# A planned decoder layer on one core: queues of tiles sorted by first use, links between real users of a tile, PSUM banks by need, and gate and value columns in one group

## The chip, the cores and the metric

The kernel runs on one core of one Trainium2 chip. The metric is the device time of one launch in microseconds. The engines are TensorE (PE), VectorE (DVE), ScalarE (ACT), GpSimd (POOL), and SyncE (SP), which issues all transfers.

## The reference, cut to what matters

One decoder layer on `x` of 2048 x 1024 float32. Two head groups share the projection `w_in`: an RG-LRU and a Conformer convolution module. Then come `w_out`, cross-attention into 256 memory tokens, and a gated FFN with a short convolution.

```python
h = rms_norm(x, mix_norm_g[l])
z = h @ w_in[l]                                   # 1024 x 2048
lru_x, lru_gate, conf_a, conf_b = jnp.split(z, [D_LRU, 2 * D_LRU, 2 * D_LRU + D_CONF], axis=-1)
lru_x = causal_dwconv(lru_x, lru_conv_w[l], lru_conv_b[l])
y_lru = rg_lru(lru_x, ...) * jax.nn.gelu(lru_gate, approximate=True)
c = conf_a * jax.nn.sigmoid(conf_b)               # value, gate
c = causal_dwconv(c, conf_conv_w[l], conf_conv_b[l])      # 31 taps
c = jax.nn.silu(layer_norm(c, conf_ln_g[l], conf_ln_b[l]))
x = x + jnp.concatenate([y_lru, c], axis=-1) @ w_out[l]
...
scores = jnp.einsum("bshd,bmhd->bhsm", q, k) * (XA_HD ** -0.5)
p = jax.nn.softmax(scores, axis=-1)
x = x + jnp.einsum("bhsm,bmhd->bshd", p, v).reshape(bsz, s, d) @ w_o[l]
...
x = x + (jax.nn.gelu(causal_dwconv(g, ...), approximate=True) * u) @ w_down[l]
return rms_norm(x, final_norm_g)
```

## The kernel before

The kernel is written as a program that is recorded first and ordered afterwards. Every operation (a matmul, a vector operation, a transfer) becomes an `Op` with an engine, an estimated cost, its predecessors, and the buffers it uses. Buffers are taken from pools: `S` (86 tiles of 128x512 in SBUF), `W` (4 wide tiles, which hold the raw weight columns `raw` among others), `D` (3 tiles for the 31-tap convolution), and `ps` (the 8 banks of PSUM). The recording order comes from generators (tasks such as `mix`, `channels`, `recurrences`, `attend`) that yield to each other.

`emit` then plans in `PASSES` rounds. `deadlines` walks the operations backwards and gives each a due time: no later than each successor's due time less the cost, and, by `extra`, no later than what the next user of the same pool slot needs. `schedule` simulates the engines forward: each engine takes the ready operation with the earliest due time, and a buffer gets a slot when one is free. The queue of each pool says whose turn is next; it stands in the order of recording. The plan with the earliest estimated end is kept, and the instructions of all engines are written in one sequence in its order. The chip runs each engine's instructions in that order. All instructions come from one helper line of `emit` (L452 before, L485 with the change), so the profile is read by the names of tiles.

Products are float32 products made of three: both operands are split into a high and a low part (`wh`, `wl`; `xh`, `xl`), and three 128x512 matmuls are added in a bank (`mm3`). The products of `w_out`, of the attention and of the FFN go by Strassen's scheme (`seven`, with the list `FIRST` for `w_out`); their combined operands are `yh`, `yl`, `s`, `Xh`, `Xl`.

The work around the change: the sequence is cut into two halves `h` of 1024 positions, of two quarters `q` of 512 each. `mix(h)` makes z for one half: `project(h, c0, put)` multiplies 256 columns of `w_in` from column `c0`, which `Columns.get` loads with `raw_cols` in two tiles of 512 rows (`kq`), and hands each finished bank to `put`. `mix_conf(h, c)` does that for the gate columns of two 128-channel blocks and then for their value columns; the sigmoid of the gate waits in `sg` tiles meanwhile, and the product goes to the DRAM tile `zc`. `channels(h)` runs the 31-tap convolution (`conv`; tiles `so`, `e`, `f`) of each channel block `c` once `got["conf", h, ...]` is done. `mix_lru` and `recurrences` do the same for the LRU (tiles `z`, `xc`, `gate`, `gelu`). `attend(h)` multiplies by `w_out`, normalises the queries and runs the softmax (tiles `prob`, `sum`, `r`, `pt`).

Of the kernel before, what the change touches and what calls it, by code (L numbers as in the profile page):

```python
# [14 lines left out]
ALU = mybir.AluOpType  # L15
AX = mybir.AxisListType

P = 128
# [35 lines left out]
ACT_SWITCH = 1.3  # L54
ACT_PATIENCE = 8.0
POOL_LAST = 6.0
PASSES = 12
BACKLOG = 4.0
EARLY_STORE = 40.0
SMALLS = 720  # L60
STACKS = 2
# [90 lines left out]

class Op:
    __slots__ = ("eng", "idx", "calls", "cost", "delay", "sets", "preds", "succs", "bufs", "due",
                 "wait", "at", "start", "either", "on", "turn", "store", "first", "early")

    def __init__(self, eng, idx):
        self.eng, self.idx = eng, idx
# [6 lines left out]
class Program:  # L165
# [94 lines left out]
    def prepare(self):  # L260

        for tag, queue in self.queues.items():
            live = []
            for b in queue:
                while live and live[0] < b.ops[0].idx:
                    heapq.heappop(live)
                heapq.heappush(live, b.ops[-1].idx)
                assert len(live) <= SLOTS[tag], tag
        for o in self.ops:
            for p in o.preds:  # L270
                p.succs.append(o)
        extra = {}
        for tag, queue in self.queues.items():
            dead = sorted(queue, key=lambda b: b.ops[-1].idx)
            for i, b in enumerate(queue[SLOTS[tag]:]):
                for u in dead[i].ops:
                    extra.setdefault(u.idx, []).append(b.ops[0])
        self.extra = extra

    def deadlines(self, order):  # L280

        t = 0.0
        for o in order:
            if o.eng == "PE":
                t = o.due = o.turn = t if o.start is None else o.start
                t += o.cost
            else:
                o.due = t + 30 if o.store else 1e9
        for o in self.ops:
            o.start, o.at = None, 0.0  # L290
        for o in reversed(self.ops):
            lat = o.cost + o.delay + HOP
            if o.early:
                o.due -= EARLY_STORE
            for s in o.succs:
                o.due = min(o.due, s.due - lat)
            for s in self.extra.get(o.idx, ()):
                if s.idx > o.idx:
                    o.due = min(o.due, s.due - lat)
            if o.first:  # L300
                o.due = o.idx - 1e6
        for _ in range(STACKS):
            for e in ("DVE", "ACT", "SP"):
                t = 1e9
                for o in sorted((o for o in self.ops if o.eng == e and not o.first), key=lambda o: -o.due):
                    t = o.due = min(o.due, t - o.cost)
            for o in reversed(self.ops):
                lat = o.cost + o.delay + HOP
                if o.eng != "PE" and not o.first:
                    for s in o.succs:  # L310
                        o.due = min(o.due, s.due - lat)

    def schedule(self):
        events, seq = [], [0]
# [8 lines left out]
        def push(t, kind, x):  # L323
            seq[0] += 1
            heapq.heappush(events, (t, seq[0], kind, x))

        def satisfied(o, t):
            o.at = max(o.at, t)
            o.wait -= 1
            if o.wait == 0:  # L330
                push(o.at, 1, o)

        def grant(tag, t):
            while free[tag] and queues[tag]:
                b = queues[tag].pop()
                b.slot = free[tag].pop(0)
                b.left = len(b.ops)
                for o in b.heads:
                    satisfied(o, t)
# [59 lines left out]

        for o in self.ops:  # L400
            o.wait = len(o.preds) + 1
        for tag, queue in self.queues.items():
            for b in queue:
                for o in b.heads:
                    o.wait += 1
        for tag in SLOTS:
            grant(tag, 0.0)
        for o in self.ops:
# [20 lines left out]
                        free[b.tag].append(b.slot)  # L429
                        grant(b.tag, t + HOP)  # L430
        assert len(order) == len(self.ops)
        self.estimated = end
        return order

    def emit(self, tc):
        self.prepare()
        best, order = None, self.ops
        for _ in range(PASSES):
            self.deadlines(order)
            order = self.schedule()  # L440
            if best is None or self.estimated < best[0]:
                best = self.estimated, order, {o.idx: (o.start, o.on) for o in order}, {id(b): b.slot for q in self.queues.values() for b in q}
        _, order, places, slots = best
        with tc.manual_schedule(engines=None):
            for o in order:
                o.start, o.on = places[o.idx]
                for b in o.bufs:
                    if b.real is None:
                        b.real = self.place(b, slots[id(b)])
                e = self.engines[o.on]  # L450
                for name, args, kw in o.calls:
                    getattr(e, name)(*[resolve(a) for a in args], **{k: resolve(a) for k, a in kw.items()})  # L452
# [27 lines left out]
def hybrid_layer(  # L480
# [44 lines left out]
    def tmp(name="tmp"):  # L525
        return pr.new("S", name=name)
# [137 lines left out]
    class Kept:  # L664
# [18 lines left out]
        def get(self, i, shape=None, name=None):  # L683
            b = pr.new("S", shape, self.dtype, name or self.name)
            self.load((b[:] if shape is None else flat(b)).f32(), i)
            return b

    def raw_cols(w, c0, kq):
        st = pr.new("W", (P, KQ, 2 * P), name="raw")
        pr.dma(st[:], w[kq * KQ * P : (kq + 1) * KQ * P, c0 : c0 + 2 * P].rearrange("(k p) f -> p k f", p=P))  # L690
        return st

    def raw_rows(w, r0):
# [13 lines left out]
    class Columns:  # L707


        def __init__(self, w, name, n, uses):  # L710
            self.w, self.kept, self.uses = w, Kept(name, n * 4) if uses > 1 else None, uses
            self.seen = {}

        def get(self, c0, kq):
            key = (c0, kq)
            n = self.seen[key] = self.seen.get(key, 0) + 1
            base = ((c0 // (2 * P)) * 2 + kq) * 4
            if n > 1:
                return [tuple(self.kept.get(base + 2 * f + i, (P, KQ, P), "w" + "hl"[i]) for i in range(2)) for f in range(2)]
            st = raw_cols(self.w, c0, kq)  # L720
            got = [split_cols(st, f) for f in range(2)]
            if n < self.uses:
                for f in range(2):
                    for i in range(2):
                        self.kept.put(base + 2 * f + i, flat(got[f][i]))
            return got
# [110 lines left out]
    def wide(name):  # L837
        return pr.new("W", (P, 2 * TT), name=name)

    got = {(n, h, c): Task(None) for n in ("conf", "lru") for h in range(NH) for c in (0, 2)}  # L840

    def project(h, c0, put):
        pp = [[ps(), ps()] for _ in range(2)]
        for kq in range(2):
            ww = W_in.get(c0, kq)
            for f in range(2):
                wh, wl = ww[f]
                for th in range(2):
                    with together():
                        for k in range(KQ):  # L850
                            x = MX[h][th][kq * KQ + k]
                            mm3(pp[f][th][:], wh[:, k, :], wl[:, k, :], x[0][:], x[1][:], kq + k == 0, kq == 1 and k == KQ - 1)
                    if kq:
                        put(f, th, pp[f][th])
                    yield 0

    def mix(h):
        parts = [mix_conf, mix_lru]
        for part in parts:
            for c in (0, 2):  # L860
                yield from part(h, c)
        mixed_in[h].done = True
        MX[h].clear()

    def mix_conf(h, c):
        sg = {}

        def gate(f, th, p):
            t = sg[f, th] = tmp("sg")
            ACT(t[:], p[:], AF.Sigmoid)  # L870

        yield from project(h, 3 * DL + c * P, gate)

        def value(f, th, p):
            t = sg[f, th]
            V("tensor_tensor", t[:], p[:], t[:], op=ALU.mult)
            zc.put(c + f, 2 * h + th, t[:])

        yield from project(h, 2 * DL + c * P, value)
        got["conf", h, c].done = True  # L880

    def mix_lru(h, c):
# [379 lines left out]
    def channels(h):  # L1262
        acc = []
        for c in range(NC4):
            yield got["conf", h, c // 2 * 2]
            out = tmp("conv"), tmp("conv")
            yield from conv(c, h, out)
            acc.append(out)
            yield 0
        for i in range(2):  # L1270
            mixed[2 * h + i] = [o[i] for o in acc]
            conf_in[2 * h + i].done = True
# [611 lines left out]
```

## Time and profile before

| | us |
|---|---|
| median of 3 runs | 2452.07 (2451.44 to 2452.39) |
| the profiled execution, its own time | 2454.62 |
| its span | 2452.8 |
| TensorE busy | 2404.8 (98%) |
| VectorE busy | 1925.6 (79%) |
| ScalarE busy | 1281.6 (52%) |
| mean granted TensorE clock | 0.993 |

The profile is of one execution. Busy times are sums over an engine's instructions; a tile's name stands for all its buffers, in the form output<-inputs. "Idle before" names what ended an engine's wait. The chain of waits is followed back from the last instruction. "SPq" is SyncE issuing a transfer.

### The profile page before, as it was taken

How to read it: one execution, taken by the hardware profiler on the slowest of the kernel's cores; microseconds unless marked ns; L12 is line 12 of the kernel's file. 1: busy time of each engine (PE TensorE's matmuls, PEld its weight loads, DVE VectorE, ACT ScalarE, POOL GpSimd, SP SyncE). 2: the span in 40 equal slices, each digit the busy share in tenths (PEclk: the TensorE clock that was granted, in tenths of full speed). 3: DMA queues.
4: the chain of work that ended last, by engine and by line, in shares of the span. 5: the costliest groups of instructions: out<-in, count | busy, mean ns of one | idle time of the engine just before them, and what ended most of it. 6: DMA issues, size and time to landing. Idle time of an engine off the chain costs nothing.

```text
span 2452.8 us, 32183 instructions
## 1 busy us (share of the span) xinstructions
PE 2404.8 (98%) x10788; PEld 1982.3 (81%) x10788; DVE 1925.6 (79%) x3231; ACT 1281.6 (52%) x2250; POOL 0.7 (0%) x6
## 2 busy tenths in 40 slices
PE   7999999999989999999999999999999999999998
PEld 6888878888767888778888888888888888888887
DVE  6489979999989646697888888988786685667666
ACT  8237677367887556675545545545454331233222
POOL 0000000000000000000000000000000000000000
PEclk9999999999989999999999999999999999999999
DMA  7998678897887967556575456654542388779774
GB/s 252 323 307 294 218 237 309 284 313 249 265 303 246 330 232 240 188 175 235 203 239 193 146 189 220 213 186 147 179 146 69 108 284 281 251 237 357 252 245 180
DMA packets 339837, 572.05 MB, mean 233 GB/s; under 512 B 32925, under 2 KB 106653, under 8 KB 339671
## 3 DMA queue, kind: packets, MB, share of 16 engines
q1 hardware_dynamic: 339670, 570.00, 68.5%
q8 instruction: 85, 1.39, 0.2%
q14 instruction: 82, 0.66, 0.1%
HBM read 385.32 MB, written 184.55 MB: 232 GB/s over the span
## 4 chain that ended last, share of the span: by engine, by line
PE 92%; DVE 3%; ACT 2%; DMA 1%; issue 1%; SPq 0%; DVEq 0%; ACTq 0%
PE ps L452 92%; ACT prob L452 1%; ACT L452 0%; DMA raw<-in_w_q_dram 0%; DVE Xl L452 0%; DVE s L452 0%; DVE acc L452 0%; DVE gate L452 0%; SPq L452 0%; DVE wl L452 0%; DVE yl L452 0%; DVE x L452 0%; DVE e L452 0%; ACT yh L452 0%; DVE conv L452 0%
## 5 line engine op out<-in xcount | busy, mean ns | idle before, releaser
L452 PE MATMUL ps<-Xh,wh 128*128 128x512 f32 x1344 | 523.9, 390 | 0.9 <-DVE gb L452 0.9
L452 PE MATMUL ps<-Xh,wl 128*128 128x512 f32 x1344 | 523.1, 389 | 0.3 <-DVE wl L452 0.3
L452 PEld LDWEIGHTS ps<-Xh,wh 128*128 128x128 f32 x1344 | 252.3, 188 | 53.7 <-issue 1.3
L452 PEld LDWEIGHTS ps<-Xh,wl 128*128 128x128 f32 x1344 | 252.3, 188 | 53.1 <-DVE wl L452 0.8
L452 PE MATMUL ps<-wh,yh 128*128 128x512 f32 x672 | 267.8, 398 | 3.2 <-ACT pt L452 2.9
L452 PE MATMUL ps<-wh,yl 128*128 128x512 f32 x672 | 264.2, 393 | 1.6 <-DVE yl L452 1.6
L452 PE MATMUL ps<-wl,yh 128*128 128x512 f32 x672 | 264.4, 393 | 0.3 <-DMA wl<-A 0.3
L452 PE MATMUL ps<-wh,hidh 128*128 128x512 f32 x672 | 261.4, 389 | 0.0
L452 PE MATMUL ps<-wl,hidh 128*128 128x512 f32 x672 | 261.4, 389 | 0.0
L452 PE MATMUL ps<-wh,hidl 128*128 128x512 f32 x624 | 242.7, 389 | 0.0
L452 DVE TENSOR_TENSOR acc<-acc,ps 128x512 f32<-128x512 f32 x192 | 128.8, 685 | 140.8 <-PE ps L452 139.6
L452 PE MATMUL ps<-Xl,wh 128*128 128x512 f32 x576 | 224.2, 389 | 1.6 <-DVE Xl L452 1.6
L452 PE MATMUL ps<-xh,wh 128*128 128x512 f32 x512 | 201.6, 394 | 0.0
L452 PE MATMUL ps<-xh,wl 128*128 128x512 f32 x512 | 199.3, 389 | 0.0
L452 PE MATMUL ps<-xl,wh 128*128 128x512 f32 x512 | 199.3, 389 | 0.0
L452 ACT ACTIVATE wh<-s 128x512 fp32r<-128x512 f32 x192 | 118.7, 628 | 127.4 <-DVE s L452 82.2
L452 ACT ACTIVATE u<-ps 128x512 f32<-128x512 f32 x144 | 85.7, 595 | 130.2 <-PE ps L452 129.1
L452 PEld LDWEIGHTS ps<-wh,yh 128*128 128x128 f32 x672 | 128.0, 191 | 30.8 <-ACT pt L452 3.1
L452 PEld LDWEIGHTS ps<-wh,yl 128*128 128x128 f32 x672 | 127.7, 190 | 29.3 <-DVE yl L452 2.2
L452 PEld LDWEIGHTS ps<-wl,yh 128*128 128x128 f32 x672 | 128.0, 190 | 27.5 <-issue 0.8
L452 DVE TENSOR_TENSOR wl<-s,wh 128x512 fp32r<-128x512 f32 x192 | 130.5, 685 | 24.4 <-ACT wh L452 17.9
L452 PE MATMUL ps<-xn,wh 128*128 128x512 f32 x384 | 149.4, 389 | 0.0
(209 smaller groups left out, 4525.4 us busy)
## 6 DMA issues: line engine op xcount, KB each, us to landing
raw<-in_w_up_dram SPq DMA_DIRECT2D x96, 512.0 KB
wh<-w_down SPq DMA_DIRECT2D x164, 256.0 KB
wl<-w_down SPq DMA_DIRECT2D x164, 256.0 KB
hid<-cv SPq DMA_DIRECT2D x48, 512.0 KB
h<-hid SPq DMA_DIRECT2D x96, 256.0 KB
w_down<-wh SPq DMA_DIRECT2D x84, 256.0 KB
x<-in_x_dram SPq DMA_DIRECT2D x64, 256.0 KB
wl<-w_out SPq DMA_DIRECT2D x56, 256.0 KB
```

Source lines behind the costliest of these rows:

```text
L452: getattr(e, name)(*[resolve(a) for a in args], **{k: resolve(a) for k, a in kw.items()})
```

## The change

The edits, in the order of the diff:

- `PASSES` goes from 12 to 28, and every eighth pass `resort` sorts the queue of each pool by the start of the earliest operation on each buffer in the plan just made.
- The links for due times through reused slots (`extra`) are taken from the plan: when a slot is given out while fewer than `SPARE` = 3 slots are free, its last user is linked to its next. Before, they were guessed from the order of recording. `deadlines` walks the last plan backwards and not the recording.
- A PSUM bank goes to the operation with the earliest due time among those that wait for nothing but a bank (`asked`), and not to the next one in the queue.
- `project` for the Conformer part multiplies 128 gate columns and the 128 value columns of the same channel block in one group. `raw_cols` fills its tile with two transfers of 128x4x128 in place of one of 128x4x256. `channels` waits for each channel block by itself.

```diff
-PASSES = 12
+PASSES = 28
+RESORT = 8
...
+SPARE = 3
...
     def deadlines(self, order):
...
-        for o in reversed(self.ops):
+        for o in reversed(order):
...
             for s in self.extra.get(o.idx, ()):
-                if s.idx > o.idx:
-                    o.due = min(o.due, s.due - lat)
+                o.due = min(o.due, s.due - lat)
...
+    def resort(self):
+
+        for queue in self.queues.values():
+            queue.sort(key=lambda b: min(o.start for o in b.ops))
...
+        def taken(b, tag):
+            b.slot = free[tag].pop(0)
+            if len(free[tag]) < SPARE and (tag, b.slot) in last:
+                for u in last[tag, b.slot].ops:
+                    extra.setdefault(u.idx, []).extend(b.heads)
+            last[tag, b.slot] = b
...
         def satisfied(o, t):
             o.at = max(o.at, t)
             o.wait -= 1
             if o.wait == 0:
                 push(o.at, 1, o)
+            elif o.wait == 1 and o.bank is not None:
+                heapq.heappush(asked, (o.due, o.idx, o))
+                grant("ps", t)
 
         def grant(tag, t):
+            if tag == "ps":
+                while free[tag] and asked:
+                    o = heapq.heappop(asked)[2]
+                    b, o.bank = o.bank, None
+                    taken(b, tag)
+                    b.left = len(b.ops)
+                    satisfied(o, t)
+                return
...
-        for _ in range(PASSES):
+        for n in range(1, PASSES + 1):
+            if n % RESORT == 0:
+                self.resort()
             self.deadlines(order)
             order = self.schedule()
...
-    def raw_cols(w, c0, kq):
+    def raw_cols(w, c0, kq, c1=None):
         st = pr.new("W", (P, KQ, 2 * P), name="raw")
-        pr.dma(st[:], w[kq * KQ * P : (kq + 1) * KQ * P, c0 : c0 + 2 * P].rearrange("(k p) f -> p k f", p=P))
+        rows = w[kq * KQ * P : (kq + 1) * KQ * P]
+        if c1 is None:
+            pr.dma(st[:], rows[:, c0 : c0 + 2 * P].rearrange("(k p) f -> p k f", p=P))
+        else:
+            for f, c in enumerate((c0, c1)):
+                pr.dma(st[:, :, f * P : (f + 1) * P], rows[:, c : c + P].rearrange("(k p) f -> p k f", p=P), join=f > 0)
...
     def mix(h):
-        parts = [mix_conf, mix_lru]
-        for part in parts:
-            for c in (0, 2):
-                yield from part(h, c)
+        for c in range(NC4):
+            yield from mix_conf(h, c)
+        for c in (0, 2):
+            yield from mix_lru(h, c)
...
-        def gate(f, th, p):
-            t = sg[f, th] = tmp("sg")
-            ACT(t[:], p[:], AF.Sigmoid)
-
-        yield from project(h, 3 * DL + c * P, gate)
-
-        def value(f, th, p):
-            t = sg[f, th]
-            V("tensor_tensor", t[:], p[:], t[:], op=ALU.mult)
-            zc.put(c + f, 2 * h + th, t[:])
-
-        yield from project(h, 2 * DL + c * P, value)
+        def gated(f, th, p):
+            if f == 0:
+                t = sg[th] = tmp("sg")
+                ACT(t[:], p[:], AF.Sigmoid)
+            else:
+                t = sg[th]
+                V("tensor_tensor", t[:], p[:], t[:], op=ALU.mult)
+                zc.put(c, 2 * h + th, t[:])
+
+        yield from project(h, 3 * DL + c * P, gated, 2 * DL + c * P)
...
     def channels(h):
         acc = []
         for c in range(NC4):
-            yield got["conf", h, c // 2 * 2]
+            yield got["conf", h, c]
```

The number of matmuls (10556), of VectorE and GpSimd instructions stays; table loads of ScalarE go from 77 to 73, and SyncE issues 8 transfers more. The order of the instructions moves on every engine. Three places follow.

SyncE, at the start: the tiles of x (`x`), of `w_kv` and `w_q` (`raw`), and the short vectors. Before, up to the second tile of `w_q`:

```order
L452 DMA x<-in_x_dram 128x512 x8
L452 DMA raw<-in_w_kv_dram 128x4x256 x2
L452 DMA x<-in_x_dram 128x512
L452 DMA raw<-in_conf_conv_w_dram 31x512
...
L452 DMA raw<-in_lru_conv_b_dram 1x512
L452 DMA x<-in_x_dram 128x512
L452 DMA raw<-in_w_q_dram 128x4x256
L452 DMA x<-in_x_dram 128x512 x6
L452 DMA raw<-in_w_q_dram 128x4x256
```

With the change, at the same place:

```order
L485 DMA x<-in_x_dram 128x512 x2
L485 DMA raw<-in_w_kv_dram 128x4x256
L485 DMA x<-in_x_dram 128x512 x5
L485 DMA raw<-in_w_kv_dram 128x4x256
L485 DMA x<-in_x_dram 128x512
L485 DMA raw<-in_w_q_dram 128x4x256
L485 DMA raw<-in_conf_conv_w_dram 31x512
...
L485 DMA raw<-in_lru_conv_b_dram 1x512
L485 DMA x<-in_x_dram 128x512 x6
L485 DMA raw<-in_w_q_dram 128x4x256
L485 DMA raw<-in_w_out_dram 128x512 x2
L485 DMA raw<-in_w_in_dram 128x4x128 x5
```

The first tile of `w_q` now stands ahead of the short vectors, and 14 tiles of x, not 16, ahead of the second.

VectorE, at the second wide reciprocal (`r`) of the queries' norm in the first attention, among the softmax sums (`s`, `smalls`) and the residual (`x`). Before:

```order
L452 RECIPROCAL smalls<-smalls 128x2 x2
L452 TENSOR_TENSOR x_5599<-x_5599,ps 128x512
L452 RECIPROCAL smalls<-smalls 128x2
L452 RECIPROCAL r<-r 128x512
L452 TENSOR_TENSOR yl<-s,yh 128x512 x2
L452 SCALAR_TENSOR_TENSOR conv<-conv,v_97,r 128x512 x4
```

With the change:

```order
L485 TENSOR_TENSOR x_5276<-x_5276,ps 128x512
L485 TENSOR_TENSOR yl<-s,yh 128x512
L485 SCALAR_TENSOR_TENSOR conv<-conv,v_97,r 128x512 x2
L485 TENSOR_TENSOR yl<-yf,yh 128x512 x2
L485 SCALAR_TENSOR_TENSOR conv<-conv,v_97,r 128x512
L485 RECIPROCAL r<-r 128x512
L485 TENSOR_TENSOR yl<-yf,yh 128x512
```

The reciprocal, which stood between the row sums of the softmax, stands behind them.

TensorE, at the sums of squares of that norm (`ps<-sum,ones`) and the transposes of the softmax (`ps<-ident,prob`). Before:

```order
L452 MATMUL ps<-sum,ones 128x512
L452 MATMUL ps<-wh,yh 128x512
L452 MATMUL ps<-wl,yh 128x512
L452 MATMUL ps<-wh,yl 128x512
L452 MATMUL ps<-wh,yh 128x512
L452 MATMUL ps<-wl,yh 128x512
L452 MATMUL ps<-wh,yl 128x512
L452 MATMUL ps<-sum,ones 128x512 x2
L452 MATMUL ps<-wh,yh 128x512
```

With the change:

```order
L485 MATMUL ps<-wh,yh 128x512
L485 MATMUL ps<-wl,yh 128x512
L485 MATMUL ps<-wh,yl 128x512
L485 MATMUL ps<-sum,ones 128x512 x2
L485 MATMUL ps<-ident,prob 128x128 x32
L485 MATMUL ps<-wh,yh 128x512
```

The last pair of sums stands later, and 32 transposes of the softmax follow it in one run, where before the last 32 stood in two runs of 16.

More of the change, by code (lines that the diff above doesn't have):

```diff
@@ L154 @@
     __slots__ = ("eng", "idx", "calls", "cost", "delay", "sets", "preds", "succs", "bufs", "due",
-                 "wait", "at", "start", "either", "on", "turn", "store", "first", "early")
+                 "wait", "at", "start", "either", "on", "turn", "store", "first", "early", "bank")
     def __init__(self, eng, idx):
@@ L276, in prepare @@
                 for u in dead[i].ops:
-                    extra.setdefault(u.idx, []).append(b.ops[0])
+                    if u.idx < b.ops[0].idx:
+                        extra.setdefault(u.idx, []).append(b.ops[0])
         self.extra = extra
@@ L325, in push @@
             heapq.heappush(events, (t, seq[0], kind, x))
+        asked, last, extra = [], {}, {}
+        def taken(b, tag):
[4 more added lines that the diff above has]
+            last[tag, b.slot] = b
         def satisfied(o, t):
@@ L331, in satisfied @@
                 push(o.at, 1, o)
+            elif o.wait == 1 and o.bank is not None:
+                heapq.heappush(asked, (o.due, o.idx, o))
+                grant("ps", t)
         def grant(tag, t):
+            if tag == "ps":
[6 more added lines that the diff above has]
+                return
             while free[tag] and queues[tag]:
                 b = queues[tag].pop()
-                b.slot = free[tag].pop(0)
+                taken(b, tag)
                 b.left = len(b.ops)
@@ L401, in schedule @@
             o.wait = len(o.preds) + 1
+            o.bank = None
         for tag, queue in self.queues.items():
@@ L405, in schedule @@
                     o.wait += 1
+                    if tag == "ps":
+                        assert o.bank is None and len(b.heads) == 1
+                        o.bank = b
         for tag in SLOTS:
@@ L431, in schedule @@
         assert len(order) == len(self.ops)
-        self.estimated = end
+        self.estimated, self.extra = end, extra
         return order
@@ L711, in __init__, with get @@
             self.w, self.kept, self.uses = w, Kept(name, n * 4) if uses > 1 else None, uses
-            self.seen = {}
-        def get(self, c0, kq):
+            self.seen, self.at = {}, {}
+        def get(self, c0, kq, c1=None):
             key = (c0, kq)
             n = self.seen[key] = self.seen.get(key, 0) + 1
-            base = ((c0 // (2 * P)) * 2 + kq) * 4
+            base = self.at.setdefault(key, 4 * len(self.at))
             if n > 1:
                 return [tuple(self.kept.get(base + 2 * f + i, (P, KQ, P), "w" + "hl"[i]) for i in range(2)) for f in range(2)]
-            st = raw_cols(self.w, c0, kq)
+            st = raw_cols(self.w, c0, kq, c1)
             got = [split_cols(st, f) for f in range(2)]
@@ L838, in wide, with project @@
         return pr.new("W", (P, 2 * TT), name=name)
-    got = {(n, h, c): Task(None) for n in ("conf", "lru") for h in range(NH) for c in (0, 2)}
-    def project(h, c0, put):
+    got = {(n, h, c): Task(None) for n in ("conf", "lru") for h in range(NH) for c in range(NC4)}
+    def project(h, c0, put, c1=None):
         pp = [[ps(), ps()] for _ in range(2)]
         for kq in range(2):
-            ww = W_in.get(c0, kq)
+            ww = W_in.get(c0, kq, c1)
             for f in range(2):
```

## The prediction

> **What bounds the kernel now.** I read the page first, then TensorE's waits, then the stages as windows, then the chain of waits at the places where TensorE waits.
>
> ```profile
> span 2452.8 us, 32183 instructions
> PE 2404.8 (98%) x10788; PEld 1982.3 (81%) x10788; DVE 1925.6 (79%) x3231; ACT 1281.6 (52%) x2250; POOL 0.7 (0%) x6
> PE 92%; DVE 3%; ACT 2%; DMA 1%; issue 1%; SPq 0%; DVEq 0%; ACTq 0%
> ```
>
> TensorE is busy for 98% of the span and is 92% of the chain that ended last. The change alters no matmul, so it can only move the time in which TensorE waits (2452.8 - 2404.8 = 48.0 us) and the time in which it runs at a lower clock after a wait. The waits by releaser (total, times, longest; us), six of the longest and one more:
>
> ```profile
> PE ps L452 <- ACT mem L452: 7.0, 2, 6.2
> PE ps L452 <- ACT prob L452: 6.8, 4, 4.6
> PE ps L452 <- DMA raw<-in_w_q_dram: 4.8, 1, 4.8
> PE ps L452 <- DVE sum L452: 4.8, 2, 2.8
> ...
> PE ps L452 <- ACT pt L452: 2.9, 1, 2.9
> ...
> PE ps L452 <- DVE Xl L452: 1.6, 1, 1.6
> PE ps L452 <- DVE x L452: 1.5, 1, 1.5
> ...
> PE ps L452 <- DVE gb L452: 0.9, 1, 0.9
> ```
>
> Where they lie shows in the stages (columns: window, length, busy time and instructions of each engine, granted clock, DMA share, GB/s):
>
> ```profile
> 0.00:185.50 185.50, 169.89 (x800) 142.25 (x801) 119.03 (x289) 92.31 (x169) 0.70 (x6) 0.98 0.87 295
> 185.50:523.00 337.50, 337.50 (x1498) 272.52 (x1498) 313.66 (x492) 219.36 (x345) 0.00 (x0) 1.00 0.82 274
> 523.00:762.00 239.00, 219.74 (x973) 176.76 (x972) 231.65 (x406) 187.99 (x353) 0.00 (x0) 0.96 0.79 268
> 762.00:1085.00 323.00, 317.66 (x1493) 264.84 (x1492) 214.80 (x381) 194.46 (x424) 0.00 (x0) 0.99 0.72 247
> 1085.00:2440.00 1355.00, 1354.69 (x6009) 1121.79 (x6008) 1037.55 (x1647) 584.20 (x951) 0.00 (x0) 1.00 0.61 206
> ```
>
> From 185 to 523 and from 1085 to 2440 us TensorE never waits, and nothing can be gained there. The largest loss is the stage 523 to 762 (first attention: products of w_out, queries' norm, softmax): TensorE waits 239.00 - 219.74 = 19.3 us there and its clock of 0.96 costs 239 x 0.04 = 9.6 more, together 28.9. In the same stage VectorE is busy for 231.65 of 239 us: it is the bound, and ScalarE, which works in turn with it, is second. Within it the clock falls after each run of waits:
>
> ```profile
> 656.00:664.00 8.00, 7.39 (x18) 5.39 (x19) 8.00 (x14) 7.07 (x10) 0.00 (x0) 0.57 0.73 264
> ...
> 723.00:727.00 4.00, 1.17 (x5) 0.44 (x3) 4.00 (x8) 3.85 (x8) 0.00 (x0) 1.00 0.98 356
> 727.00:735.00 8.00, 6.00 (x13) 3.66 (x12) 7.37 (x18) 7.82 (x18) 0.00 (x0) 0.57 0.64 229
> ```
>
> **The change part by part. First term, VectorE's ledger in the stage 523 to 762.** The instructions of all engines are written in one sequence, and in the trace of before VectorE runs beside TensorE as written. So I count what is written for VectorE ahead of the same matmul, in before and after. Ahead of the first product of w_out (matmul 2068 of the program, at 523 us): 774 instructions before, 787 after. Ahead of the end of the softmax stretch (matmul 3039, at 762 us): 1176 before, 1177 after. Between the two VectorE has 402 to do before and 390 after, while TensorE has the same 971 matmuls. The cause is the earlier first convolution: its first VectorE row stands behind 104 us of TensorE work in place of 120 (matmuls written ahead of it, each by its shape's time in the trace), since gate and value of one channel block are now one group and the convolution waits for one block, not two. By kind the twelve are ten scalar_tensor_tensor, one tensor_tensor and one 512-column reciprocal (the second one of the queries' norm, now written after the softmax). Their prices:
>
> ```profile
> L452 DVE TENSOR_TENSOR x<-x,ps 128x512 f32<-128x512 f32 x36 | 23.4, 677 | 0.0
> L452 DVE SCALAR_TENSOR_TENSOR f<-so,fast,f 128x512 f32<-128x512 f32 x22 | 16.4, 743 | 0.0
> ...
> L452 DVE RECIPROCAL r<-r 128x512 f32<-128x512 f32 x2 | 6.7, 3339 | 0.0
> ```
>
> 10 x 0.743 + 0.677 + 3.339 = 11.4 us; run back to back, as in the chain, a scalar_tensor_tensor takes 0.66 and a tensor_tensor 0.60, which makes 10.5. I take 10.5, since VectorE has no gaps there. It lies on the path: VectorE is what TensorE waits for. The thirteen instructions that move ahead of 523 us cost 13 x 313.66/492 = 8.3 us of VectorE in a stage where it has 337.50 - 313.66 = 23.8 us free and TensorE waits for nothing: that cover hides them. If it were gone, TensorE would lose up to 8.3 us there. Ends for this term: 0, if the waits are ScalarE's alone (prob 6.8 us of the 19.3), and 28.9, the whole loss.
>
> ScalarE has 18 table loads between the two matmuls after, and 26 before, at 1.28 us each by the chain:
>
> ```profile
> 655.88 0.68 DVE xl L452
> ...
> 656.61 46.74 PE ps L452 x199
> 703.35 2.43 ACT prob L452 x9
> ...
> 727.84 1.28 ACT L452
> ```
>
> That is 8 x 1.28 = 10.2 us less for an engine that is busy for 187.99 of 239 us. It shares the path with VectorE, so I count it at 0 beside the 10.5 and keep it for a rival. What is late next in this stage, where VectorE then still has 231.65 - 10.5 = 221 us against TensorE's 239 - 28.9 = 210: VectorE again, at the softmax sums. The table loads moved ahead of 523 us, 4 more, are 5.1 us in a stage where ScalarE has 118 us free: 0.
>
> **Second term, 1062 to 1085 us.** VectorE works without a gap here, and TensorE waits for it at the end (Xl 1.6 and gb 0.9 us):
>
> ```profile
> 1062.43 0.68 DVE s L452
> ...
> 1079.94 1.81 DVE xn L452 x3
> 1081.75 0.61 DVE gb L452
> ...
> 1082.50 17.72 PE ps L452 x81
> ```
>
> Ahead of the first product of the FFN (matmul 4444) 1524 VectorE instructions are written after, 1519 before: 5 x 0.6 = 3.0 us of head start against waits of 2.5. I take 2.5; ends 0 and 3.0. The wait for pt at 991 us keeps its order: 0.
>
> **Third term, the start.** TensorE waits 4.84 us for the second w_q tile, whose transfer is queued behind x tiles on SP's queue:
>
> ```profile
> 23.78 8.68 DMA raw<-in_w_q_dram
> ...
> 32.59 27.57 PE ps L452 x130
> ```
>
> SP's queue now holds 14 x tiles ahead of it and not 16: 2 x 0.262 MB less. Rate and cost of a packet, first from 22 to 34 us, then from 2000 to 2100 us:
>
> ```profile
> DMA packets 3378, 3.82 MB, mean 318 GB/s; under 512 B 707, under 2 KB 2478, under 8 KB 3375
> q1 hardware_dynamic: 3375, 3.78, 102.0%
> ```
>
> ```profile
> q1 hardware_dynamic: 15571, 28.88, 86.4%
> ```
>
> 0.524 MB at 318 GB/s is 1.65 us earlier, and I take 1.7. Ends: -2.0 (SP is held once more by a full queue; two issues took it 2.42 us at 29.13) and 4.84.
>
> ```profile
> 23.78 0.41 SPq L452 DMA_DIRECT2D raw<-in_w_q_dram  x1
> ...
> 29.13 2.42 SPq L452 DMA_DIRECT2D raw<-in_w_out_dram  x2
> ```
>
> The clock after this wait was 0.66:
>
> ```profile
> 30.00:40.00 10.00, 7.41 (x25) 6.41 (x26) 5.43 (x39) 8.82 (x21) 0.00 (x0) 0.66 1.03 284
> ```
>
> The Trainium skill ("TensorE: Matmul & The Clock Gate", What's actually happening) says that the clock drops only after an idle window of about 3.4 us. By that rule a wait of 4.84 - 1.7 = 3.1 us would keep the clock, and 10 x 0.34 = 3.4 us would be gained on top, 2434 in place of 2437. This trace doesn't bear it out: waits of at most 2.83 us with TensorE busy for 1.17 of 4 us (723 to 727) were followed by 0.57. I keep the ramp in the sum and give the rule a share of the gaining rival.
>
> **What costs nothing.** More passes, the sorting and the links are done while the program is built; on the chip only their order counts, and it is in the ledger. Column tiles: sixteen transfers of 512-B pieces in place of eight of 1024-B pieces for the same 4.2 MB. The two packet rows give 12 x 16 x 1.02/3375 = 58 ns at 1120 B and 100 x 16 x 0.864/15571 = 89 ns at 1855 B; the line through them 32.5 ns at 512 B and 54 at 1024, so 8192 x 32.5/16 - 4096 x 54/16 = 2.8 us of all queues, with ends 0 (by bytes) and 4096 x 58/16 = 14.8 (a short piece costs as much as these). Eight more issues hold SP for 8 x 0.41 = 3.3 us. Both are hidden behind the lead of the tiles: the first product of w_in is moved from behind 24.8 us of TensorE work to behind 17.9, and its later tiles are issued 20 us of TensorE work or more ahead of their use. If that cover is gone, up to 18 us go on the path. Banks by need: the same 8 banks; TensorE switches between groups about 26 times from 293 to 357 us, where it now waits for nothing.
>
> **Sum.** 10.5 + 2.5 + 1.7 = 14.7 us. The profiled execution took 2454.62 us, so 2439.9; the median of the runs is 2.55 below it, so 2437.4.
>
> **Rivals.**
> (A) The head start is taken back by transfers. The row 50 to 100 us speaks for it, with the DMA engines at 0.95:
>
> ```profile
> 50.00:100.00 50.00, 50.00 (x238) 41.39 (x237) 33.19 (x72) 24.03 (x42) 0.00 (x0) 1.00 0.95 331
> ```
>
> Late w_in tiles would then hold TensorE for up to 14.8 + 3.3 us; against it, TensorE never waited there. Time: 2437 + 15 to 18 = 2452 to 2455, no change. Chance 0.13.
> (B) Slower: banks by need. A bank goes to the group that is due, so two groups of products mix and TensorE waits at the switches for the operand of the second. For it: a switch with a late operand costs 1.55 us (the wait for x, above). Against: before has such switches without waits. At 26 switches it takes back all from 14.7/26 = 0.57 us each; at 0.9 us it gives 2437 + 23 = 2460. Chance 0.09.
> (C) More gain: the relief of ScalarE adds to VectorE's, or the clock holds. 10.2 x 0.8 (its busy share) = 8 us more gives 2429. For it: prob carries 6.8 us of the waits. Against: the same softmax is still one chain after another. Chance 0.09.
> (D) Only half of the first term comes: VectorE's surplus sits in two humps, and the second reciprocal is only moved behind the softmax, where the next wait may take it. 2437 + 5 to 8 = 2442 to 2445. Chance 0.14; still faster.
> That the change does not do what it says is excluded by the order of the instructions, which differs.
>
> **How the numbers follow.** The forecast has 0.55. Faster by over 0.2% (4.9 us, about what a measurement of this kernel can tell from no change): 0.55 + 0.14 + 0.09 = 0.78. Same: 0.13. Slower: 0.09. The range leaves out what lies beyond (C), about 0.05, and (B) and the upper half of (A), 0.15: 2429 to 2452.
>
> **What would show it.** Right: VectorE with about 221 us of work between the same matmuls, and TensorE's waits there down from 19.3 to about 11 us; no waits for Xl and gb near 1065; the wait for w_q about 3 us; matmuls without a wait from 185 to 510. Wrong: a wait on raw<-in_w_in before 200 us (A), several of 0.5 us or more between 290 and 360 us (B), or waits for prob and sum that still make 13 us (D).

## The result and the profile after

The changed kernel takes 2434.44 us (median of six runs, 2432.39 to 2436.44), the kernel before 2452.23 us in the same comparison (2451.34 to 2453.93). The ratio is 0.9925, 95% interval 0.9914 to 0.9936: 17.8 us less. The profiled execution took 2434.40 us, 20.2 less than the one of before. The head of the page:

```profile
span 2432.6 us, 32495 instructions
PE 2399.2 (99%) x10788; PEld 1979.2 (81%) x10788; DVE 1923.1 (79%) x3231; ACT 1278.8 (53%) x2246; POOL 0.7 (0%) x6
```

The same 10788 matmul records; TensorE now waits for 2432.6 - 2399.2 = 33.4 us in place of 48.0, and is busy for 5.6 us less, since fewer of its matmuls ran at a lower clock. TensorE's waits (engine, what it waited for: total, times, longest, in us):

```profile
PE ps L485 <- ACT mem L485: 7.2, 2, 6.5
PE ps L485 <- ACT prob L485: 4.5, 1, 4.5
PE ps L485 <- ACT pt L485: 3.4, 2, 2.9
...
PE ps L485 <- ACT r L485: 2.8, 2, 2.1
PE ps L485 <- DVE prob L485: 1.1, 2, 0.6
PE ps L485 <- ACT x L485: 1.1, 1, 1.1
PE ps L485 <- DVE x L485: 0.8, 2, 0.6
PE ps L485 <- ACT yh L485: 0.6, 2, 0.4
```

The waits for w_q, sum, Xl and gb are gone. In windows (window, length, busy time and count of each engine, granted clock, DMA share, GB/s), from the first product of w_out to the end of the softmax stretch, then the place of the late stall:

```profile
519.00:638.60 119.60, 114.30 (x534) 94.14 (x532) 119.60 (x194) 87.83 (x151) 0.00 (x0) 1.00 0.84 285
638.60:745.00 106.40, 101.11 (x446) 81.14 (x447) 102.66 (x204) 90.06 (x197) 0.00 (x0) 0.95 0.75 260
```

```profile
1040.00:1085.00 45.00, 45.00 (x206) 37.37 (x205) 43.17 (x74) 34.22 (x64) 0.00 (x0) 1.00 0.47 154
```

From 519 to 745 us TensorE waits for (119.60 - 114.30) + (106.40 - 101.11) = 10.6 us, 19.3 before. The stretch lasts 226 us, 239 before. VectorE is still busy for all of the first 119.60 us, and for 222.3 us of the 226. By what ended them, 10.3 us of the waits before were put down to VectorE and 8.4 to ScalarE; now it is 1.9 and 8.5. So the waits that went are those for VectorE, and most that are left end on ScalarE's tiles (prob, r, pt, yh). Around 1077 us TensorE no longer waits.

To place the 20.2 us I compare the start of each matmul with the usual distance to the next start of its shape (0.227 us for 128x512, 0.109 for 128x128); what is above it is lost time, waits and slow clock together. Up to 60 us of TensorE work before lost 21.7 us and after 17.7: 4.0 gained at the start. From 500 to 760 us of TensorE work it was 33.0 and 18.8: 14.2 gained (by the windows above, 13 us). From 760 to 1100 us 8.0 and 6.4: 1.6 gained; a stall of 0.7 us at 1528 us is gone; small differences elsewhere take 0.3 back.

### The profile page after: what moved, and what is told of

The parts are those of the page before. It is cut to its first block, busy times and chain, and to the rows that moved or that the text cites. A ratio compares the mean times of both kernels' runs of the same rounds, so it can differ in the third digit from the quotient of the medians.

```text
span 2432.6 us, 32495 instructions
## 1 busy us (share of the span) xinstructions
PE 2399.2 (99%) x10788; PEld 1979.2 (81%) x10788; DVE 1923.1 (79%) x3231; ACT 1278.8 (53%) x2246; POOL 0.7 (0%) x6
## 3 DMA queue, kind: packets, MB, share of 16 engines
q8 instruction: 85, 1.39, 0.2%
## 4 chain that ended last, share of the span: by engine, by line
PE 71%; ACT 3%; DVE 1%; issue 0%; DMA 0%; DVEq 0%; ACTq 0%
PE ps L485 71%; ACT prob L485 2%; ACT yh L485 0%; ACT L485 0%; ACT pt L485 0%; DVE yl L485 0%; DVE acc L485 0%; DMA VO<-VO 0%; DVE smalls L485 0%; DMA VO<-yh 0%; DVE conv L485 0%; DVE gate L485 0%; DVE prob L485 0%; ACT m L485 0%; ACT sq L485 0%
## 5 line engine op out<-in xcount | busy, mean ns | idle before, releaser
L485 PE MATMUL ps<-tx,wh 128*128 128x512 f32 x384 | 149.4, 389 | 0.0
```

## The experiments

**Theory** after the result: VectorE's ledger. In the stretch between 350 and 760 us of TensorE work VectorE has about as much to do as TensorE, and an order is as good as it keeps VectorE's surplus from piling up. **Rivals**: ScalarE's table loads and softmax bound the stretch; or the planner's new rules alone earn the gain; or the banks cost waits. For the start, the rivals are named with the runs.

### The planner alone, and the grouping alone

`planner_only`: all changes of the planner, columns as before.

```diff
-    for c in range(NC4):
-        yield from mix_conf(h, c)        # gate and value of one block in one group
+    for c in (0, 2):
+        yield from mix_conf(h, c)        # gates of two blocks, then their values
```

> The changed planner (passes, sorting, links, banks) with the columns of w_in grouped as before. Theory (VectorE's ledger): counted in the written order, VectorE's surplus over TensorE between 377 and 724 us of TensorE work grows to 37 us (before 34, changed kernel 24), so TensorE loses some 4 us more there than before; the start keeps its 4 us (the first w_q tile is issued ahead of the short vectors) and the late stage its 2: 2452 - 6 + 4 = 2450 us, 2446 to 2454. Rival (the planner's rules earn the gain, the grouping little): 2434 to 2439 us.

Measured: 2450.49 us, ratio to before 0.9994 (0.9985 to 1.0003); here and below, distances to the changed kernel are to its 2434.44 us. The theory's number; the rival falls. The parts fit as well: in the traces the stretch loses 5 us more than before (4 expected), the start 4.7 less (4), and the part from 760 to 1100 us of TensorE work 4.5 less (2). Where the surplus peaks, VectorE is busy for 38.90 of 40 us and TensorE for 29.25:

```profile
680.00:720.00 40.00, 29.25 (x116) 20.13 (x114) 38.90 (x74) 24.54 (x55) 0.00 (x0) 0.87 0.50 166
```

Transfers take part too: 6.9 us of TensorE's waits in the stretch end on tiles that are loaded again (`wh<-VO`, `wl<-VO`). The chain of waits behind one of them runs on VectorE, from 707 to 714 us, before the transfer is issued; behind the last it runs on ScalarE's softmax, from 730 to 745 us.

`group_only`: the planner of before, with the new columns (the same lines the other way round, in the kernel before).

> The planner of before with gate and value columns in one group. Theory (VectorE's ledger): surplus 29 us against 34 before, so 4.7 us gained between 523 and 762; nothing gained at the start (the first w_q tile stays behind the short vectors) nor at 1077 us: 2447.5 us, 2445 to 2451. Rival (ScalarE bounds that stretch: its own surplus goes from 21.7 before to 10.0): 11.7 us gained, 2440.5 us.

Measured: 2460.99 us, ratio 1.0031 (1.0019 to 1.0043), slower than before. Both numbers were wrong. The windows show why:

```profile
420.00:470.00 50.00, 50.00 (x222) 41.42 (x221) 50.00 (x81) 11.53 (x19) 0.00 (x0) 1.00 0.84 282
470.00:500.00 30.00, 30.00 (x135) 24.82 (x134) 30.00 (x49) 18.13 (x27) 0.00 (x0) 1.00 0.73 242
...
550.00:575.00 25.00, 12.12 (x36) 8.53 (x35) 25.00 (x42) 9.39 (x15) 0.00 (x0) 0.73 0.38 111
575.00:650.00 75.00, 74.53 (x361) 62.18 (x360) 68.75 (x117) 64.80 (x113) 0.00 (x0) 1.00 0.93 309
```

VectorE is busy without a gap from 420 to 575 us, first while TensorE does not wait, then, from 550 us on, with TensorE waiting for half of the time, 9.33 us for one x tile; afterwards it has 6.25 us free. ScalarE is busy for 9.39 of the 25 us, so it is no ScalarE stall. One figure for the surplus was too coarse: the work comes in humps, VectorE cannot work ahead in the gap between them, and each hump is paid for. So I kept the ledger from both sides: along the written order VectorE's surplus never falls below 0, and what goes above 3 us is waiting of TensorE. (The 3 us were chosen on the runs up to act_add.) From 350 to 760 us of TensorE work, beside the time lost in the traces:

| kernel | ledger, us | lost in the trace, us |
|---|---|---|
| before | 32.4 | 32.8 |
| changed | 21.9 | 19.1 |
| planner_only | 37.3 | 38.0 |
| group_only | 32.9 | 36.5 |
| no_links | 32.1 | 32.5 |
| no_bank | 24.3 | 21.3 |
| dve_add | 31.7 | 32.4 |
| act_add | 22.3 | 25.0 |
| sort9 (counted ahead of the run) | 17.8 | 21.3 |
| after_exp | 21.9 | 18.2 |

It is within 3.7 us for all ten: enough to tell 21 from 33, not 18 from 21. That is a fit more than a test. The rule and its 3 us were found on eight of these runs, after_exp leaves VectorE's order as it is, and sort9, the one order counted ahead, was put below the changed kernel and came out above it. The prices of VectorE's instructions matter as well: with the mean of each shape where it runs back to back in the traces, the ledger comes out 2 to 5 us lower, in nearly the same order.

### The links and the banks undone

```diff
-        self.estimated, self.extra = end, extra
+        self.estimated = end
```

> The changed kernel without the links between real users of a slot: the links guessed from the order of recording stay. Theory (VectorE's ledger): surplus 30.0 us against 24.3 in the changed kernel, start unchanged: 2434.4 + 5.7 = 2440 us, 2437 to 2444. Rival (ScalarE's surplus decides, 11.6 against 15.5): 2434.4 - 4 = 2430.5 us.

Measured: 2447.84 us, ratio to before 0.9980 (0.9970 to 0.9990), 13 us above the changed kernel. The direction is the theory's, the size is beyond its range, and the two-sided ledger, made afterwards, has it (32.1 for 32.5). The longest wait, 9.15 us, is put down to ScalarE's yh, but ScalarE was busy for 5.72 of those 14 us and VectorE for all:

```profile
548.00:562.00 14.00, 4.85 (x19) 3.25 (x18) 14.00 (x22) 5.72 (x9) 0.00 (x0) 0.80 0.24 78
```

For the banks, `grant` and `satisfied` go back to the queue:

```diff
-            elif o.wait == 1 and o.bank is not None:
-                heapq.heappush(asked, (o.due, o.idx, o))
-                grant("ps", t)
```

> The changed kernel with PSUM banks in queue order. Theory (VectorE's ledger): surplus 26.9 us against 24.3, and the first w_q tile is again issued behind the short vectors, 1 to 2 us at the start: 2434.4 + 2.6 + 1.5 = 2438.5 us, 2435 to 2442. Rival (banks by need make TensorE wait at switches between groups): faster than the changed kernel, 2425 to 2432 us.

Measured: 2439.50 us, ratio 0.9943 (0.9926 to 0.9960), as expected in the total, and no sign of a cost of banks by need. In the traces 3.9 us are lost at the start (21.2 by 40 us of TensorE work against 17.3), where 1.5 were expected, and 2.3 in the stretch (2.6 expected); 1.4 come back behind it.

The passes alone were not run: with 28 passes and nothing else the kernel before keeps its order to the last instruction. The sorting was not undone by itself.

### VectorE or ScalarE, by 16 more instructions each

```diff
+                    if 2100 <= pe < 2500 and more and args and args[0].buf.name in ("yl") and o.on == "DVE":
...
-                    getattr(e, name)(...)
+                    for _ in range(twice):
+                        getattr(e, name)(...)
```

> The changed kernel with 16 VectorE instructions written twice (yl<-s,yh, 128x512, 0.60 to 0.69 us each, the same result), behind the first 2100 matmuls, where the stretch that loses time begins: 9.6 to 11 us more VectorE work. Theory (VectorE bounds the stretch, it was busy for 119.60 of the 119.60 us from 519 us on): the whole comes on top, 2434.4 + 10 = 2444.5 us, 2442 to 2447. Rival (ScalarE's table loads and softmax bound it): at most 2 us more, 2434 to 2437 us.

Measured: 2445.51 us, ratio to before 0.9971 (0.9959 to 0.9983), 11.1 above the changed kernel for 9.6 to 11 us of work. The wait appears where the added work ends, for an x tile of VectorE (0.20 us there in the changed kernel):

```profile
600.53 0.79 PE L493 MATMUL ps<-xh,gwah 128*128 128x512 f32 x1 [8.40 <-DVE x L493]
```

`act_add` has "yh" and "ACT" in the same lines.

> The changed kernel with 16 ScalarE instructions written twice (yh, 128x512, 0.53 to 0.63 us each, the same result) at the same place: 8.5 to 10 us more ScalarE work. Theory (VectorE bounds the stretch; ScalarE was busy for 87.8 of 119.6 us there): at most 2 us more, 2434 to 2437 us. Rival (ScalarE bounds it): 2434.4 + 9 = 2443.5 us.

Measured: 2439.86 us, ratio 0.9946 (0.9931 to 0.9961), 5.4 above the changed kernel: between the two. VectorE is the bound in this part, but it works in turn with ScalarE. Added ScalarE work makes VectorE wait:

```profile
519.00:560.00 41.00, 40.37 (x183) 32.34 (x182) 39.64 (x66) 29.93 (x47) 0.00 (x0) 1.00 0.81 272
560.00:600.00 40.00, 37.65 (x162) 30.70 (x161) 38.28 (x62) 29.18 (x56) 0.00 (x0) 0.96 0.90 306
600.00:645.00 45.00, 40.45 (x199) 33.45 (x198) 44.27 (x71) 40.12 (x69) 0.00 (x0) 0.96 0.74 243
```

It is idle for 1.36 + 1.72 + 0.73 = 3.8 us here, and for none up to 638 us in the changed kernel; what VectorE loses comes on top.

### The start

Three edits of SyncE's order in the kernel before, each nothing else. That of start_x is shown; start_hole moves sp[29] ahead of sp[19], and start_tail moves sp[37] and sp[38] ahead of sp[45] in the same way.

```diff
+        sp = [o for o in order if places[o.idx][1] == "SP"]
+        order = [o for o in order if o is not sp[36]]      # start_x: the second w_q tile
+        order.insert(order.index(sp[34]), sp[36])          # goes ahead of two x tiles
```

> The kernel before with the second w_q tile moved ahead of two x tiles in SyncE's queue, and nothing else. The prediction's step: 0.52 MB less ahead of it at 318 GB/s, 1.65 us earlier, wait 3.2 us: 2452.2 - 1.7 = 2450.5 us. The rule of the clock gate (a wait under 3.4 us keeps the clock): 3 us more on top, 2447.5 us. Rival: the two x tiles come late instead and the wait only changes its name: 2452 us.

Measured: 2452.02 us, ratio 0.9998 (0.9988 to 1.0007): the rival. TensorE's wait for the tile ended at 30.11 in place of 32.59, 2.5 us earlier where the step says 1.65, but TensorE then waited 2.15 us for copies of the transposed tile (`qt`), and the clock still fell:

```profile
30.11 1.06 PE L455 MATMUL ps<-ident,raw 128*128 128x128 f32 x8 [1.84 <-DMA raw<-in_w_q_dram]
33.33 2.93 PE L455 MATMUL ps<-kv,qt 128*128 128x256 f32 x6 [2.15 <-ACT qt L455]
```

```profile
30.00:40.00 10.00, 7.74 (x25) 6.22 (x26) 4.96 (x30) 9.57 (x21) 0.00 (x0) 0.66 1.08 296
```

The rival has the number, but not the reason. The x tiles are not late: ScalarE waited 0.23 us for one, 0.40 before. It ran without a gap from 26.22 us on, and the copies stand in its order behind its work on x (`junk`, the squares, and `xh`):

```profile
31.58 0.60 ACT L455 ACTIVATE qt<-ps 128x512 f32<-128x512 f32 x1
32.67 0.60 ACT L455 ACTIVATE qt<-ps 128x512 f32<-128x512 f32 x1
```

So the next wait was for ScalarE's order, which this edit does not touch.

> The kernel before with the first w_q tile issued ahead of the nine short vectors, not behind them, and nothing else; the bytes ahead of the second w_q tile stay the same. The prediction's step (bytes ahead of the tile decide): no change, 2452.2 us. Theory now: the transfer engines stand nearly empty from 15 to 20 us, while the short vectors are fetched, and 0.52 MB moved into that hole make everything behind it 1.65 us earlier: wait about 3.2 us, 2450.5 us (2447.5 if the clock then holds).

Measured: 2453.51 us, ratio 1.0002 (0.9993 to 1.0012), and the wait grew from 4.84 to 6.42 us. The hole theory falls: the short vectors behind the moved tile come later, and all that follows them. SyncE issues the last one at 21.07 us (19.63 before), and the second w_q tile at 24.64 (23.78).

```profile
33.93 1.94 PE L455 MATMUL ps<-ident,raw 128*128 128x128 f32 x8 [6.42 <-DMA raw<-in_w_q_dram]
```

> The kernel before with the first two loads of the gates' weights (256-byte pieces), which stand right behind the second w_q tile in SyncE's queue, moved seven places down, and nothing else; they are read at 48 us. Theory now (what is issued right behind a tile shares the transfer engines with it and delays its landing, 8.7 us here): the tile lands 2 to 3 us earlier, wait about 2.5 us, 2449.5 us (2446.5 if the clock then holds). The prediction's step (only what is queued ahead of it counts): no change, 2452.2 us.

Measured: 2452.53 us, ratio 1.0000 (0.9991 to 1.0009). The wait went from 4.84 to 3.65 us and ended 0.8 us earlier, at 31.80 in place of 32.59; TensorE came to it 0.4 us later. If the loads issued right behind the tile cost it anything, it is 0.8 us, not 2 to 3, and the total can't tell it. One execution can't either: with one and the same order at the start, the wait for this tile ended at 30.71 us in after_exp, and in the changed kernel the tile was there by 29.89.

```profile
31.80 1.94 PE L456 MATMUL ps<-ident,raw 128*128 128x128 f32 x8 [3.65 <-DMA raw<-in_w_q_dram]
```

No single edit gives the 4.0 us of the changed kernel. There the second w_q tile has fewer x tiles ahead, other loads behind, and TensorE's own work is in another order: it waits twice briefly, for x and xl, and not for w_q (after_exp, with the same order there, waited 1.38 us for it), and the clock stays.

```profile
27.38 1.09 PE L485 MATMUL ps<-ident,x 128*128 128x128 f32 x8 [1.07 <-ACT x L485]
28.74 1.31 PE L485 MATMUL ps<-ident,x 128*128 128x128 f32 x8 [0.27 <-DVE xl L485]
```

```profile
30.00:40.00 10.00, 9.64 (x47) 7.68 (x46) 8.03 (x20) 8.20 (x20) 0.00 (x0) 1.00 1.11 334
```

ScalarE's order is another too. Its eight squares of x, of which seven stood ahead of the first copy of qt before, now stand behind the first two copies (28.94 us); the other two come at 37.22 and 38.31 us, while TensorE already has products of w_in to do (the first at 34.43 us, 46.73 before). The squares, before and with the change (count: shortest, median and longest in ns, first and last start):

```profile
L452 ACT ACTIVATE junk<-x x8: 617/626/634, 23.3 to 31.7; 128x512 f32<-128x512 f32 x8
L485 ACT ACTIVATE junk<-x x8: 617/623/625, 36.6 to 44.4; 128x512 f32<-128x512 f32 x8
```

How the 4.0 us divide among these was not tried.

### The pieces of the column tiles

```diff
+                    if o.idx in self.wide:                  # the second transfer of a tile
+                        if self.wide[o.idx] is None:
+                            continue                        # is left out, the first loads 256 columns
```

> The changed kernel with each of the eight tiles of gate and value columns loaded by one transfer of 256 neighbouring columns (1024-byte pieces), as before, in place of two of 128 (512-byte pieces): the value columns are then not the right ones, the order and the work are the same. Theory (the pieces and the eight more issues are hidden): 2434.4 us, within 1.5. Rival (they cost some of their 2.8 us of transfers and 3.3 us of SyncE at the start): 2429 to 2432 us.

Measured: 2433.32 us, ratio to before 0.9920 (0.9907 to 0.9934), 1.1 below the changed kernel, whose own interval overlaps. The 512-byte pieces and the eight more issues are hidden to within what this measurement tells.

### Two tries for a faster version

`sort9`: RESORT = 9.

> The changed kernel with the queues sorted every ninth pass, not every eighth: another order out of the same planner. Theory (VectorE's ledger, kept from both sides: VectorE cannot work ahead of TensorE, and TensorE waits once VectorE is 3 us behind): between 350 and 760 us of TensorE work it gives 32.4 us of waiting for the kernel before (32.8 in the trace), 21.9 for the changed one (19.1 in the trace) and 17.8 for this one: 2434.4 - 4.1 = 2430.3 us, 2427 to 2433.5. Rival (the ledger only fits the runs it was made from): no relation, as likely above 2434.4 as below.

Measured: 2436.04 us, ratio to before 0.9933 (0.9920 to 0.9947): the expected gain did not come. The stretch lost 21.3 us, not 17.8. Its waits there end on both engines (ScalarE's yh, r, pt and prob 4.8 us, VectorE's prob, x and xl 6.4), and the ledger sees only VectorE. A difference of 4 us between two such orders is beyond it.

`after_exp`:

```diff
+        a, b = ups[28:30]                      # exponential and tanh of one gate tile
+        order.remove(b)
+        order.insert(order.index(a) + 1, b)
```

> The changed kernel with one ScalarE instruction (tanh of the gate) moved four places up behind the exponential of the same tile, so that two of the four table loads ahead of the longest wait (4.54 us for prob, at 638 us) fall away: 2.6 us less ScalarE work just where TensorE waits for ScalarE. Theory (VectorE, busy for all of 519 to 638 us, bounds the stretch): the wait is shorter there and comes back later, 2434.4 us, at most 0.8 less. Rival (ScalarE's table loads bound it at that place): 2434.4 - 2.6 = 2431.8 us.

Measured: 2431.94 us, ratio to before 0.9915 (0.9901 to 0.9928). By the total the rival is right; by the trace it is neither. The wait of 4.54 us at 638 us became two:

```profile
636.21 0.67 PE L489 MATMUL ps<-wh,yh 128*128 128x512 f32 x1 [2.27 <-ACT prob L489]
642.59 0.51 PE L489 MATMUL ps<-wh,yh 128*128 128x512 f32 x1 [1.08 <-ACT prob L489]
```

So 1.2 of the 2.6 us were gained there, and 0.9 over the stretch. Most of the rest in the profiled execution lies elsewhere: behind the same wait of 2.89 us near 976 us the clock was 0.69 for ten microseconds in the changed kernel and 1.00 here.

```profile
976.60:986.60 10.00, 9.93 (x31) 7.90 (x32) 9.46 (x19) 10.00 (x26) 0.00 (x0) 0.69 0.24 58
```

```profile
975.60:985.60 10.00, 9.91 (x44) 8.18 (x45) 9.90 (x20) 10.00 (x26) 0.00 (x0) 1.00 0.44 133
```

It has the lowest median, but its interval overlaps the changed kernel's; that it is faster stays open.

## Why the prediction was right, point by point

- **The bound and the place.** The gain came from the three places named, with 0.7 us more at 1528 us, and nothing was lost elsewhere: no waits from 185 to 519 us, none from 1060 us to the tail. VectorE has 222.3 us of work in the stretch, 221 were forecast. What is late next there was wrong: not VectorE at the softmax sums, but for the most part ScalarE (8.5 of 10.6 us).
- **First term, 10.5 us; measured 14.2 (13 by the windows).** The waits fell by 19.3 - 10.6 = 8.7 us, less than forecast. What was left out is the clock: 239 x 0.04 = 9.6 us of it were lost before, and 106.4 x 0.05 = 5.3 after, so 4.3 came on top. The prediction had these 9.6 us in its account of the loss and no part of them in the gain. So the two errors go against each other, and the total is nearer than its terms.
- **The step of this term, from the count to the time.** Twelve fewer VectorE instructions between two matmuls were priced and taken as time. The same count in the written order of the other runs, with the time from the first product of w_out to the 971st matmul record behind it in the trace, doesn't bear this out:

| kernel | VectorE instructions between | time in the trace, us |
|---|---|---|
| before | 402 | 239.0 |
| changed | 390 | 224.2 |
| group_only | 382 | 242.6 |
| planner_only | 413 | 243.1 |
| no_links | 395 | 236.2 |
| no_bank | 394 | 227.5 |
| sort9 | 383 | 226.9 |

group_only has twenty fewer and gains nothing: its work stands in a hump, TensorE waits for 12.9 us of the 25 from 550 us on, and the time that VectorE has free afterwards does not give them back. So the grouping does lower the count, as the prediction says, but the count alone does not give the time, and that it did so here is in part luck. That VectorE's work is on the path in the first part of the stretch was shown by dve_add (11.1 us for 9.6 to 11). That the gain needs both parts was shown by planner_only and group_only. That it comes from where VectorE's work piles up is what the ledger says; it was fitted to these runs and failed its one test.

- **ScalarE's relief at 0.** Perhaps too low; it was not tried by itself. act_add shows that work added to ScalarE counts for about half (5.4 us for 8.5 to 10), since VectorE waits for it. In after_exp, 2.6 us less of it gained 0.9 us over the stretch.
- **Second term, 2.5 us.** The waits for Xl and gb went, and lost time there fell by 3.2 us (the clock was 1.00 there before, too); the unchanged wait for pt at 976 us lost 1.5 us more to the clock this time. Net 1.6.
- **Third term, 1.7 us; measured 4.0.** The step (bytes ahead of the tile) may be right for the tile itself: in start_x its wait ended 2.5 us earlier for the same 0.52 MB, in one execution. But the same run gained nothing, so the step from the tile to the time failed: an earlier tile alone only uncovered the next wait, ScalarE's qt. The changed kernel moves TensorE's and ScalarE's work there as well; that this is why it gained is argued, not tried.
- **The rule of the clock gate** (the Trainium skill, "TensorE: Matmul & The Clock Gate", What's actually happening: an idle window of about 3.4 us). The number it gave, 2434, is the measured one, and the clock after the start was 1.00. Neither bears the rule out: the start gave 4.0 us and not 1.7 + 3.4, the rest of the total came from the stretch, and in start_x two waits of 1.84 and 2.15 us, each under 3.4, with work between them, left the clock at 0.66. What the traces show in its place stands at the end.
- **Rivals.** (A) fell: TensorE waits for no w_in tile, and wide_dma moves the time by 1.1 us. (B) fell: banks in queue order are 5 us slower, and TensorE did not wait between 290 and 360 us. (C) is open in part: the gain is above the forecast by the clock, and a share of ScalarE's in it isn't shown. (D) fell as a number (the waits for prob make 5.6 us and those for sum are gone, not 13), but the two humps that it names are what group_only paid for.

## What to carry to other kernels

When a planner's rules move everything, count for the same landmarks how much work of the second-busiest engine is written ahead, and keep the count from both sides: work that it could have done earlier does not fill a later hump. The net count between two places is not enough, since the work between them can stand in a hump. Changes that are worth nothing or less alone (the planner's rules -2.7 us by the medians, not clear of no change; the grouping +7.8) can be worth 17.8 together. Our reading, which no run shows by itself, is that the grouping makes work available early and the rules decide where it goes. So undo parts from the whole before judging them. A transfer that is moved forward alone may only show the next wait, as in start_x.

## What the runs showed of the hardware

- The same wait of 2.89 us cost between 0.1 us (after_exp, no_links) and 3.0 us (the changed kernel) of slow clock behind it. The runs of the changed kernel spread over 4.05 us; it is a reason not to read a difference of 2 us in one execution.
- What decides this is where the wait falls. In all fourteen traces the granted clock is 1.00 or 0.50, and it changes only at the ends of intervals of 3.41 us, whose grid stays fixed within an execution. In the changed kernel 2.20 us of the wait fell into one interval, and the clock was 0.50 for the next two; in after_exp the wait was split into 1.50 and 1.39 us, and the clock stayed:

```profile
972.58:975.99 3.41, 1.21 (x12) 0.96 (x9) 3.41 (x6) 3.41 (x11) 0.00 (x0) 1.00 0.22 77
975.99:982.82 6.83, 6.14 (x15) 4.79 (x16) 6.25 (x15) 6.83 (x19) 0.00 (x0) 0.50 0.32 79
```

```profile
970.89:974.30 3.41, 1.91 (x17) 1.67 (x15) 3.41 (x6) 3.41 (x9) 0.00 (x0) 1.00 0.17 37
974.30:977.71 3.41, 2.02 (x9) 1.67 (x10) 2.84 (x6) 3.41 (x11) 0.00 (x0) 1.00 0.11 43
977.71:984.54 6.83, 6.83 (x32) 5.65 (x31) 6.80 (x16) 6.83 (x18) 0.00 (x0) 1.00 0.54 160
```

Between 20 and 2400 us the fourteen traces have 192 intervals at full clock in which TensorE was idle for over 0.3 us. All 46 that were idle for more than 0.58 of their length were followed by an interval at 0.50, and none of the 133 that were idle for less than 0.49; of the 13 between, some were and some were not.

- Waits of 1.4 to 1.5 us at the start (after_exp, planner_only) left the clock at 1.00, 2.43 us (no_links) at 0.83, and 1.84 and 2.15 us with 1.1 us between them (start_x) at 0.66, over 30 to 40 us.
